# RWKV-7 recurrence in a hybrid decoder layer: V products on 64 rows, alternated with U and Y products of the preceding chunk

## The chip, the cores and the metric

The kernel runs on one core of a Trainium2 chip. The metric is the device time of one execution in microseconds. PE is TensorE (PEld its weight loads), DVE VectorE, ACT ScalarE, POOL GpSimd, and SP the engine whose queue issues most transfers.

## What is computed

One decoder layer on 1024 tokens of width 1024: a SwiGLU block, a mixer of two parallel groups of eight heads (stick-breaking attention and RWKV-7 time mixing), and a second SwiGLU block, each between RMS norms. The change lies in the RWKV-7 recurrence:

```python
def rwkv7_scan(r, w, k, v, a_vec, b_vec):
    """State S_h (N_v, N_k):
    S_t = S_{t-1} diag(w_t) + (S_{t-1} a_t) b_t^T + v_t k_t^T ;  y_t = S_t r_t."""
...
    def step(state, inp):
        r_t, w_t, k_t, v_t, a_t, b_t = inp
        sa = jnp.einsum('bhij,bhj->bhi', state, a_t)
        state = (state * w_t[:, :, None, :]
                 + sa[..., None] * b_t[:, :, None, :]
                 + v_t[..., None] * k_t[:, :, None, :])
        y = jnp.einsum('bhij,bhj->bhi', state, r_t)
        return state, y
```

## The kernel before

The layer runs in stages: first SwiGLU block, input projections, then the recurrence together with most of the attention, output projection with the rest of the attention, second SwiGLU block.

The recurrence does not step token by token. The 1024 tokens are cut into 16 chunks of 64 (`ch`, four to a quarter `q`). Earlier stages have written to DRAM, for each chunk, the operands A (`a_d`), M (`m_d`), B transposed (`bt_d`), a solved triangular matrix (`tt_d`) and the values V (`vt_d`). `chain_load(ch)` brings four of them in, three buffers each, on SP's queue. In the tile `UV` rows 64 to 127 are V, and rows 0 to 63 are set to zero by GpSimd (L1217) and later filled with U.

`rw_chain(q)` then does, for each chunk, with heads in four pairs `pr` of two heads `hd`:

1. V products (L1265): eight matmuls of M (128 rows, 128 columns as weights) with UV, 64 columns each, into the PSUM bank `gy`. UV's first 64 rows are zero at this time.
2. A products (L1268): four matmuls of A with the state S, added onto the same bank; then GpSimd scales the state (`sw`, L1271).
3. ScalarE copies gy's first 64 partitions to G (L1273).
4. U products (L1277): eight 64x64 matmuls of TT with G into a bank `us`; ScalarE copies the result to UV's first 64 rows (L1279).
5. S products (L1282): four matmuls of B with the whole of UV into another bank `us`; VectorE adds `sw` and writes the new state (L1286).
6. Y products (L1289): eight 64x64 matmuls of M's first 64 rows with U, added onto gy's last 64 partitions; ScalarE copies them out (L1292).

Each float32 matmul appears in the trace as two passes, each a weight load (LDWEIGHTS) and a MATMUL.

`rw_post(q)`, once per quarter, normalises the outputs and transposes them through two banks `us` (L1316), which VectorE reads (L1319). Attention (`att_s1` to `att_s4`: Z products L1392, mask L1395, transposes L1418, O products L1430) is written between the chunks by `pull`. A scheduler then orders each engine's instructions by its own estimate of when they are ready; `keep_in_program_order` ties an instruction behind the one written before it on its engine. Each engine runs its instructions in that fixed order.

PSUM has eight banks, given out by `PB_`: gy 1, us 2, z 2, at 2, po 1. `pcol` and `pc` pick the columns of a head or a pair of heads.

Of the kernel before, what the change touches and what calls it, by code (L numbers as in the profile page):

```python
# [30 lines left out]
def layer_kernel(ctx: ExitStack, tc: tile.TileContext, a: dict, out: bass.AP, dbg=None):  # L31
    nc = tc.nc
# [44 lines left out]
    def bank(tag, name):  # L77
        return PS.p.tile([P, 512], F32, tag=tag, name=name, bufs=PS.bufs[tag])
# [652 lines left out]
    v_d = dr.tile([T, 512], F32, name="v_d")  # L731
    yh_d = dr.tile([D, T], F32, name="yh_d")
    yl_d = dr.tile([D, T], F32, name="yl_d")
    PB_ = dict(gy=1, us=2, z=2, at=2, po=1)
    a_d = dr.tile([16, P, 4, P], F32, name="a_d")
    m_d = dr.tile([16, P, 4, 2, P], F32, name="m_d")
    bt_d = dr.tile([16, P, 4, P], F32, name="bt_d")
    tt_d = dr.tile([16, 64, 4, P], F32, name="tt_d")
# [129 lines left out]

    pm = Pool("ms", dict(qk=3, tmp=1, sl=1, L=1, TT=1))
    pl = Pool("ma", dict(t2=14, e65=4, ab=2, M=2))  # L870
    C4 = 4
# [143 lines left out]
    def rw_build(q, h):  # L1015
        pr, AB = q.pr, q.AB[h]
        odd = pr % 2
        if h == 0:
            if not odd:
                slabs[0] = pm.tile("sl", f"slab{pr}", [P, 32, 32])  # L1020
                slabs[1] = pm.tile("TT", f"TT{pr}", [P, 32, 64])
        bk = []
# [45 lines left out]
    def rw_solve(qs):  # L1068
        u = qs[0].pr
        slab, TT = slabs  # L1070
        L = pm.tile("L", f"L{u}", [P, 32, 32])
# [12 lines left out]
        nc.vector.transpose(TN, L.rearrange("p i j -> p j i"))  # L1084
        nc.vector.transpose(TT[:, :, 0:32].rearrange("p r i -> p i r"), L)
        for i in range(2):
            nc.gpsimd.memset(TT[kb[i][1], :, 32:64], 0.0)
        yield 6.0
        for hf in range(2):
            h16 = slice(hf * 16, hf * 16 + 16)  # L1090
            rr = range(hf * 16, hf * 16 + 16)
            for i in range(2):
                k0_, k1_ = kb[i]
                psy = bank("A", f"psy{u + i}{hf}")
                for x_, r in enumerate(rr):
                    nc.tensor.matmul(psy[k1_, x_ * 32:(x_ + 1) * 32], lhsT=TT[k0_, r, 32:64], rhs=TN[k0_, :, r],
                                     start=True, stop=True)
# [79 lines left out]
    for pr in range(4):  # L1177
        q = Pair()
# [23 lines left out]
    pb = Pool("mb", dict(A=3, M=3, bt=3, UV=3, TT=3, G=2, sw=2, Y=4, yg=3))  # L1202
# [3 lines left out]
    chain = {}  # L1206

    def chain_load(ch):
        cn = f"ch{ch}"
        A_ = pb.t2(cn + "A", [P, 4, P], tag="A")  # L1210
        nc.sync.dma_start(A_, a_d[ch])
        M = pb.t4(cn + "M", [P, 4, 2, P], tag="M")
        nc.sync.dma_start(M, m_d[ch])
        BT = pb.tile("bt", cn + "bt", [P, 4, P])
        nc.sync.dma_start(BT, bt_d[ch])
        UV = pb.tile("UV", f"{cn}UV", [P, 512])
        nc.gpsimd.memset(UV[0:64], 0.0)  # L1217
        nc.sync.dma_start(UV[64:128], vt_d[ch * 64:(ch + 1) * 64, :])
        chain[ch] = A_, M, BT, UV

    for ch in range(3):
        chain_load(ch)
# [3 lines left out]
    XP[0].close()  # L1226
    PS.open("psb", PB_)
    pa = Pool("at", dict(qk=6, V=1, p2=9, b2=3, O=2), "right")
# [15 lines left out]
    pcol = lambda pr, hd: slice(pr * P + hd * 64, pr * P + (hd + 1) * 64)  # L1244
    pc = lambda pr: slice(pr * P, (pr + 1) * P)

    def rw_chain(q):
        q.Y = pb.t4(q.nm + "Y", [P, 2, 512], tag="Y")
        for c in range(C4):
            S, Sn = S2[SCUR[0]], S2[1 - SCUR[0]]  # L1250
            SCUR[0] = 1 - SCUR[0]
            cn = f"{q.nm}c{c}"
            ch = q.qd * C4 + c
            if ch not in chain:
                chain_load(ch)
            A_, M, BT, UV = chain.pop(ch)
            TT = pb.tile("TT", cn + "TT", [64, 4, 2, 64])
            nc.sync.dma_start(TT[0:32].rearrange("p r h e -> p r (h e)"), tt_d[ch, 0:32])
            for o in range(2):
                nc.sync.dma_start(TT[32:64, :, :, o * 32:o * 32 + 32].rearrange("p r h e -> p (r h) e"),  # L1260
                                  tt_d[ch, 32:64].rearrange("p r (h o e) -> p (r h) o e", h=2, o=2)[:, :, 1 - o, :])
            gy = bank("gy", cn + "gy")
            for pr in range(4):
                for hd in range(2):
                    nc.tensor.matmul(gy[:, pcol(pr, hd)], lhsT=M[:, pr, hd, :], rhs=UV[:, pcol(pr, hd)],  # L1265
                                     start=pr == 0 and hd == 0, stop=True, skip_group_check=True)
            for pr in range(4):
                nc.tensor.matmul(gy[:, pc(pr)], lhsT=A_[:, pr, :],  # L1268
                                 rhs=S[:, pr, :], start=False, stop=True, skip_group_check=True)
            sw = pb.tile("sw", cn + "sw", [P, 4, P])  # L1270
            nc.gpsimd.tensor_tensor(sw, S, WC[:, :, ch:ch + 1].broadcast_to([P, 4, P]), op=ALU.mult)  # L1271
            G = pb.tile("G", cn + "G", [64, 512])
            nc.scalar.copy(G, gy[0:64, :])  # L1273
            u = bank("us", cn + "u")
            for pr in range(4):
                for hd in range(2):
                    nc.tensor.matmul(u[0:64, pcol(pr, hd)], lhsT=TT[:, pr, hd, :],  # L1277
                                     rhs=G[:, pcol(pr, hd)], start=True, stop=True)
            nc.scalar.copy(UV[0:64, :], u[0:64, :])  # L1279
            s = bank("us", cn + "s")  # L1280
            for pr in range(4):
                nc.tensor.matmul(s[:, pc(pr)], lhsT=BT[:, pr, :], rhs=UV[:, pc(pr)], start=True, stop=True)  # L1282
            sv = s.rearrange("p (r e) -> p r e", e=P)
            for hd in range(2):
                o = slice(hd * 64, (hd + 1) * 64)
                nc.vector.tensor_tensor(Sn[o, :, o], sv[o, :, o], sw[o, :, o], op=ALU.add)  # L1286
            for pr in range(4):
                for hd in range(2):
                    nc.tensor.matmul(gy[64:128, pcol(pr, hd)], lhsT=M[0:64, pr, hd, 64:128],  # L1289
                                     rhs=UV[0:64, pcol(pr, hd)], start=False, stop=True, skip_group_check=True)  # L1290
            ys = slice((c % 2) * 64, (c % 2) * 64 + 64)
            nc.scalar.copy(q.Y[ys, c // 2, :], gy[64:128, :])  # L1292
            yield 5.0
# [36 lines left out]
    def rwkv():  # L1330
        qs = []
        for qd in range(4):
            q = Quarter()
            q.qd, q.nm = qd, f"w{qd}"
            qs.append(q)
        for qd in range(4):
            for c, w in enumerate(rw_chain(qs[qd])):
                yield w
                if c == 0 and qd > 0:
                    yield from rw_post(qs[qd - 1])  # L1340
        yield from rw_post(qs[3])
# [243 lines left out]
```

## Time and profile before

| what | value |
| --- | --- |
| median of 3 runs | 2215.29 us (2211.8 to 2218.39) |
| the profiled execution | 2211.98 us |
| its span in the trace | 2210.3 us |
| PE busy | 2094.5 us (95%) |
| DVE, ACT, POOL busy | 1329.6, 817.2, 1108.3 us |
| mean granted PE clock | 0.976 of full speed |
| the recurrence | about 1120 to 1375 us of the span |

Busy times are sums of the durations of an engine's instructions; passes of PE overlap one another, so the pace of a group is read from where the next one starts. Times in the trace count from the span's start. The groups of rows that are used stand below.

### The profile page before, as it was taken

Reading aid. Unit: us, or ns where it says so; the run is one execution under the profiler, and the core shown is the slowest. Engines: PE = TensorE matmul, PEld = TensorE weight load, DVE = VectorE, ACT = ScalarE, POOL = GpSimd, SP = SyncE. Lnnn points to the kernel's source line nnn. Section 1 sums busy time; section 2 is a strip of 40 time slices with the busy share of each in tenths; the row PEclk is TensorE's granted clock in tenths of the full one; section 3 lists DMA queues with packets and bytes.
Section 4 is the critical chain, followed back from the end, with each engine's and each line's share of the span. In section 5 each row is a group of like instructions: output and inputs, shape, how many; then the busy total and the mean of one; then the engine's idle time right before and its main releaser. Section 6 shows DMA issues by size and latency. Waiting matters only on the chain.

```text
span 2210.3 us, 30206 instructions
## 1 busy us (share of the span) xinstructions
PE 2094.5 (95%) x10976; PEld 1719.9 (78%) x10976; DVE 1329.6 (60%) x1873; ACT 817.2 (37%) x1412; POOL 1108.3 (50%) x897
## 2 busy tenths in 40 slices
PE   8899999989999999999999999898799999998998
PEld 6678888868887777687888887777678888877886
DVE  7667777624546545735537778546676767733556
ACT  5233333332105533324136667436323333332102
POOL 2866666658542345245211111221686666647734
PEclk9999999999999999999989999999899999999999
DMA  5244555568764355164665572443235555566765
GB/s 153 76 124 130 164 141 157 153 213 307 225 215 146 78 168 172 48 181 140 192 150 159 174 217 87 157 129 115 76 100 149 161 153 146 160 225 204 254 212 190
DMA packets 415476, 353.82 MB, mean 160 GB/s; under 512 B 35169, under 2 KB 337249, under 8 KB 415329
## 3 DMA queue, kind: packets, MB, share of 16 engines
q1 hardware_dynamic: 406800, 347.45, 52.3%
q10 hardware_dynamic: 8528, 4.46, 0.9%
q8 instruction: 87, 1.43, 0.3%
q14 instruction: 61, 0.49, 0.1%
HBM read 224.96 MB, written 126.88 MB: 159 GB/s over the span
## 4 chain that ended last, share of the span: by engine, by line
PE 76%; DVE 9%; issue 4%; ACT 4%; POOL 4%; DMA 2%; SPq 0%; DVEq 0%; ACTq 0%; POOLq 0%
PE pj L124 3%; PE pj L126 2%; PE pj L125 2%; PE f2X L124 2%; PE f1X L124 2%; PE f2X L125 2%; PE f2X L126 2%; PE f1X L126 2%; PE f1X L125 2%; PE a_512o L1430 2%; PE f2DY L125 2%; PE f1DY L125 2%; PE f2DY L124 2%; PE f1DY L126 2%; PE f2DY L126 2%
## 5 line engine op out<-in xcount | busy, mean ns | idle before, releaser
L112 POOL TENSOR_SCALAR wh<-wr 128x1024 fp32r<-128x1024 f32 x54 | 62.3, 1155 | 280.1 <-PE wod L126 66.1
L319 POOL TENSOR_TENSOR f1wl<-f1r,f1wh 128x512 fp32r<-128x512 f32 x100 | 141.2, 1424 | 15.9 <-ACT f1wh L316 12.7
L319 POOL TENSOR_TENSOR f2wl<-f2r,f2wh 128x512 fp32r<-128x512 f32 x100 | 139.3, 1406 | 13.0 <-ACT f2wh L316 9.7
L113 POOL TENSOR_TENSOR wl<-wr,wh 128x1024 fp32r<-128x1024 f32 x54 | 136.6, 2532 | 3.1 <-PE pj L126 0.2
L318 POOL TENSOR_SCALAR f2wh<-f2r 128x512 fp32r<-128x512 f32 x60 | 68.5, 1147 | 107.4 <-PE f2pX L125 38.8
L318 POOL TENSOR_SCALAR f1wh<-f1r 128x512 fp32r<-128x512 f32 x60 | 60.0, 1005 | 91.6 <-PE f1X L125 27.0
L511 DVE TENSOR_TENSOR f1acc<-f1dX,f1acc 128x512 f32<-128x512 f32 x64 | 44.3, 692 | 76.8 <-PE f1dX L126 76.8
L511 DVE TENSOR_TENSOR f2acc<-f2dX,f2acc 128x512 f32<-128x512 f32 x64 | 44.3, 692 | 76.5 <-PE f2dX L126 76.5
L1409 POOL TENSOR_SCALAR a_0B<-a_512B 128x1 f32<-128x1 f32 x32 | 15.4, 482 | 131.4 <-DVE a_512B L1410 98.8
L124 PE MATMUL pj<-x1X4h,wh 128*128 128x512 f32 x176 | 75.5, 429 | 0.5 <-DVE tw L925 0.5
L124 PE MATMUL pj<-x1X2h,wh 128*128 128x512 f32 x176 | 72.3, 411 | 0.6 <-DVE qkl L1120 0.5
L126 PE MATMUL pj<-x1X4h,wl 128*128 128x512 f32 x176 | 70.5, 401 | 0.0
L125 PE MATMUL pj<-x1X4l,wh 128*128 128x512 f32 x176 | 69.6, 396 | 0.0
L125 PE MATMUL pj<-x1X2l,wh 128*128 128x512 f32 x176 | 69.4, 395 | 0.0
L126 PE MATMUL pj<-x1X2h,wl 128*128 128x512 f32 x176 | 69.4, 394 | 0.0
L319 POOL TENSOR_TENSOR f1wl<-f1S,f1wh 128x512 fp32r<-128x512 f32 x40 | 63.1, 1587 | 1.6
L319 POOL TENSOR_TENSOR f2wl<-f2S,f2wh 128x512 fp32r<-128x512 f32 x40 | 62.4, 1569 | 1.7
L537 POOL TENSOR_TENSOR f2dwl<-f2B,f2dwh 128x1024 fp32r<-128x1024 f32 x20 | 47.6, 2406 | 20.0 <-ACT f2dwh L536 20.0
L537 POOL TENSOR_TENSOR f1dwl<-f1B,f1dwh 128x1024 fp32r<-128x1024 f32 x20 | 47.6, 2401 | 19.4 <-ACT f1dwh L536 19.4
L124 PE MATMUL wod<-wh,ymh 128*128 128x512 f32 x128 | 51.6, 403 | 1.1 <-DVE woacc L196 1.1
L126 PE MATMUL wod<-wh,yml 128*128 128x512 f32 x128 | 50.2, 395 | 0.6 <-DMA yml<-yl_d 0.6
L125 PE MATMUL wod<-wl,ymh 128*128 128x512 f32 x128 | 50.4, 394 | 0.0
(1448 smaller groups left out, 7098.7 us busy)
## 6 DMA issues: line engine op xcount, KB each, us to landing
f1ho<-f1hs_d SPq DMA_DIRECT2D x112, 256.0 KB, 4.6
f2ho<-f2hs_d SPq DMA_DIRECT2D x112, 256.0 KB, 4.0
f1hs_d<-f1h SPq DMA_DIRECT2D x56, 256.0 KB, 3.3
f1hs_d<-f1l SPq DMA_DIRECT2D x56, 256.0 KB, 3.0
f2hs_d<-f2h SPq DMA_DIRECT2D x56, 256.0 KB, 3.0
f2hs_d<-f2l SPq DMA_DIRECT2D x56, 256.0 KB, 2.9
wr<-in_w_in_dram SPq DMA_DIRECT2D x27, 512.0 KB, 3.9
f1r<-in_ffn_w_gate_dram SPq DMA_DIRECT2D x19, 512.0 KB, 4.9
```

The costliest lines, as they stand in the source:

```text
L112: nc.gpsimd.tensor_scalar(wh, raw, 1.0, 0.0, op0=ALU.mult, op1=ALU.add)
L113: nc.gpsimd.tensor_tensor(wl, raw, wh, op=ALU.subtract)
L124: nc.tensor.matmul(ps, lhsT=lh, rhs=rh, start=first, stop=False, **kw)
L125: nc.tensor.matmul(ps, lhsT=lh, rhs=rl, start=False, stop=False, **kw)
L126: nc.tensor.matmul(ps, lhsT=ll, rhs=rh, start=False, stop=last, **kw)
L318: nc.gpsimd.tensor_scalar(wh, src[n], 1.0, 0.0, op0=ALU.mult, op1=ALU.add)
L319: nc.gpsimd.tensor_tensor(wl, src[n], wh, op=ALU.subtract)
L511: nc.vector.tensor_tensor(quarter(tt, n), ps, quarter(tt, n), op=ALU.add)
L537: nc.gpsimd.tensor_tensor(wl, src[n], wh, op=ALU.subtract)
L1409: nc.gpsimd.tensor_scalar(B[:, w:w + 1], iv, 1.0, 0.0, op0=ALU.mult, op1=ALU.add)
L1430: nc.tensor.matmul(po[:, 0:P], lhsT=t.AT[:, k * P:(k + 1) * P], rhs=V[:, t.z0 // P + k, :], start=t.first and k == 0, stop=t.last and k == ...
```

## The change

V products use V's 64 rows and M's rows 64 to 127 alone, so UV's first 64 rows need not be zero and the memset goes. Opening a chunk (loads, gy bank, V products) becomes a generator, `rw_open`. While chunk `ch` issues its U products, the first, third, fifth and seventh are each followed by one V product of chunk `ch + 1`, and so again with its Y products. V lies on rows 64 to 127, U and Y products on rows 0 to 63. `pin` holds this order. Chunk 0 has its V products ahead, as before. gy gets two banks, us one.

```diff
--- before.py
+++ after.py
@@ -731,7 +731,7 @@
     v_d = dr.tile([T, 512], F32, name="v_d")
     yh_d = dr.tile([D, T], F32, name="yh_d")
     yl_d = dr.tile([D, T], F32, name="yl_d")
-    PB_ = dict(gy=1, us=2, z=2, at=2, po=1)
+    PB_ = dict(gy=2, us=1, z=2, at=2, po=1)
     a_d = dr.tile([16, P, 4, P], F32, name="a_d")
     m_d = dr.tile([16, P, 4, 2, P], F32, name="m_d")
     bt_d = dr.tile([16, P, 4, P], F32, name="bt_d")
@@ -1214,7 +1214,6 @@
         BT = pb.tile("bt", cn + "bt", [P, 4, P])
         nc.sync.dma_start(BT, bt_d[ch])
         UV = pb.tile("UV", f"{cn}UV", [P, 512])
-        nc.gpsimd.memset(UV[0:64], 0.0)
         nc.sync.dma_start(UV[64:128], vt_d[ch * 64:(ch + 1) * 64, :])
         chain[ch] = A_, M, BT, UV
 
@@ -1244,26 +1243,41 @@
     pcol = lambda pr, hd: slice(pr * P + hd * 64, pr * P + (hd + 1) * 64)
     pc = lambda pr: slice(pr * P, (pr + 1) * P)
 
+    ops = {}
+    pin = tc.keep_in_program_order
+    hd8 = [(pr, hd) for pr in range(4) for hd in range(2)]
+
+    def rw_open(ch):
+
+        cn = f"ch{ch}"
+        if ch not in chain:
+            chain_load(ch)
+        A_, M, BT, UV = chain.pop(ch)
+        TT = pb.tile("TT", cn + "TT", [64, 4, 2, 64])
+        nc.sync.dma_start(TT[0:32].rearrange("p r h e -> p r (h e)"), tt_d[ch, 0:32])
+        for o in range(2):
+            nc.sync.dma_start(TT[32:64, :, :, o * 32:o * 32 + 32].rearrange("p r h e -> p (r h) e"),
+                              tt_d[ch, 32:64].rearrange("p r (h o e) -> p (r h) o e", h=2, o=2)[:, :, 1 - o, :])
+        gy = bank("gy", cn + "gy")
+        ops[ch] = A_, M, BT, UV, TT, gy
+        for j, (pr, hd) in enumerate(hd8):
+            i = nc.tensor.matmul(gy[:, pcol(pr, hd)], lhsT=M[64:128, pr, hd, :], rhs=UV[64:128, pcol(pr, hd)],
+                                 start=j == 0, stop=True, skip_group_check=True)
+            if ch:
+                pin(i)
+            yield
+
     def rw_chain(q):
         q.Y = pb.t4(q.nm + "Y", [P, 2, 512], tag="Y")
         for c in range(C4):
             S, Sn = S2[SCUR[0]], S2[1 - SCUR[0]]
             SCUR[0] = 1 - SCUR[0]
+            ch = q.qd * C4 + c
             cn = f"{q.nm}c{c}"
-            ch = q.qd * C4 + c
-            if ch not in chain:
-                chain_load(ch)
-            A_, M, BT, UV = chain.pop(ch)
-            TT = pb.tile("TT", cn + "TT", [64, 4, 2, 64])
-            nc.sync.dma_start(TT[0:32].rearrange("p r h e -> p r (h e)"), tt_d[ch, 0:32])
-            for o in range(2):
-                nc.sync.dma_start(TT[32:64, :, :, o * 32:o * 32 + 32].rearrange("p r h e -> p (r h) e"),
-                                  tt_d[ch, 32:64].rearrange("p r (h o e) -> p (r h) o e", h=2, o=2)[:, :, 1 - o, :])
-            gy = bank("gy", cn + "gy")
-            for pr in range(4):
-                for hd in range(2):
-                    nc.tensor.matmul(gy[:, pcol(pr, hd)], lhsT=M[:, pr, hd, :], rhs=UV[:, pcol(pr, hd)],
-                                     start=pr == 0 and hd == 0, stop=True, skip_group_check=True)
+            if ch not in ops:
+                for _ in rw_open(ch):
+                    pass
+            A_, M, BT, UV, TT, gy = ops.pop(ch)
             for pr in range(4):
                 nc.tensor.matmul(gy[:, pc(pr)], lhsT=A_[:, pr, :],
                                  rhs=S[:, pr, :], start=False, stop=True, skip_group_check=True)
@@ -1272,10 +1286,14 @@
             G = pb.tile("G", cn + "G", [64, 512])
             nc.scalar.copy(G, gy[0:64, :])
             u = bank("us", cn + "u")
-            for pr in range(4):
-                for hd in range(2):
-                    nc.tensor.matmul(u[0:64, pcol(pr, hd)], lhsT=TT[:, pr, hd, :],
+            ahead = rw_open(ch + 1) if ch < 15 else iter(())
+            for j, (pr, hd) in enumerate(hd8):
+                i = nc.tensor.matmul(u[0:64, pcol(pr, hd)], lhsT=TT[:, pr, hd, :],
                                      rhs=G[:, pcol(pr, hd)], start=True, stop=True)
+                if j:
+                    pin(i)
+                if j % 2 == 0:
+                    next(ahead, None)
             nc.scalar.copy(UV[0:64, :], u[0:64, :])
             s = bank("us", cn + "s")
             for pr in range(4):
@@ -1284,10 +1302,15 @@
             for hd in range(2):
                 o = slice(hd * 64, (hd + 1) * 64)
                 nc.vector.tensor_tensor(Sn[o, :, o], sv[o, :, o], sw[o, :, o], op=ALU.add)
-            for pr in range(4):
-                for hd in range(2):
-                    nc.tensor.matmul(gy[64:128, pcol(pr, hd)], lhsT=M[0:64, pr, hd, 64:128],
+            for j, (pr, hd) in enumerate(hd8):
+                i = nc.tensor.matmul(gy[64:128, pcol(pr, hd)], lhsT=M[0:64, pr, hd, 64:128],
                                      rhs=UV[0:64, pcol(pr, hd)], start=False, stop=True, skip_group_check=True)
+                if j:
+                    pin(i)
+                if j % 2 == 0:
+                    next(ahead, None)
+            for _ in ahead:
+                pass
             ys = slice((c % 2) * 64, (c % 2) * 64 + 64)
             nc.scalar.copy(q.Y[ys, c // 2, :], gy[64:128, :])
             yield 5.0
```

PE, chunk 4 (quarter 1, chunk 0) before: U (`w1c0u`), attention (names with `a_`), S and Y.

```order
L1277 MATMUL w1c0u<-w1c0G,w1c0TT 64x64 x8
L1430 MATMUL a_3_0o<-a00v,a_3_0AT 128x128 x2
L1392 MATMUL a_5_0z<-a01kh_d_9576,a01q 128x512
L1392 MATMUL a_5_0z<-a01kl_d_9579,a01q 128x512
L1282 MATMUL w1c0s<-ch4UV,ch4bt 128x128 x4
L1289 MATMUL w1c0gy<-ch4UV,ch4M 64x64 x8
L1418 MATMUL a_4_0t<-ident,a_4_0be 128x128 x4
```

The V products of chunk 5 come later, ahead of its A products:

```order
L1418 MATMUL a_6_0t<-ident,a_6_0be 128x128 x4
L1265 MATMUL w1c1gy<-ch5UV,ch5M 128x64 x8
L1268 MATMUL w1c1gy<-S_8460,ch5A 128x128 x4
L1316 MATMUL w0py_9981<-ident,w0Y 128x128 x4
L1430 MATMUL a_6_512o<-a00v,a_6_512AT 128x128 x3
L1316 MATMUL w0py_9987<-ident,w0Y 128x128 x4
```

PE, the same chunk after the change, from the last U products on; `ch5gy` with `ch5UV` is V of chunk 5.

```order
L1291 MATMUL w1c0u<-w1c0G,ch4TT 64x64 x2
L1264 MATMUL ch5gy<-ch5UV,ch5M 128x64
L1291 MATMUL w1c0u<-w1c0G,ch4TT 64x64
L1453 MATMUL a_3_0o<-a00v,a_3_0AT 128x128 x2
L1415 MATMUL a_5_0z<-a01kh_d_9594,a01q 128x512
L1415 MATMUL a_5_0z<-a01kl_d_9597,a01q 128x512
L1300 MATMUL w1c0s<-ch4UV,ch4bt 128x128 x4
L1306 MATMUL ch4gy<-ch4UV,ch4M 64x64
L1264 MATMUL ch5gy<-ch5UV,ch5M 128x64
L1306 MATMUL ch4gy<-ch4UV,ch4M 64x64 x2
```

Eight U products in a row have become single ones and pairs with a V product of chunk 5 (64 rows, which the row does not show; 128x64 is its output) between them, and the Y products likewise.

PE, the A products of chunk 5 after the change, with the transposes of the post step of quarter 0 (`w0py`) behind them:

```order
L1441 MATMUL a_6_0t<-ident,a_6_0be 128x128 x4
L1282 MATMUL ch5gy<-S_8460,ch5A 128x128 x4
L1339 MATMUL w0py_9997<-ident,w0Y 128x128 x4
L1453 MATMUL a_6_512o<-a00v,a_6_512AT 128x128 x3
L1415 MATMUL a_0_0z<-a10kh_d_10017,a10q 128x256
L1415 MATMUL a_0_0z<-a10kl_d_10020,a10q 128x256
L1339 MATMUL w0py_10003<-ident,w0Y 128x128 x4
```

The V products are gone from ahead of the A products, and two Z products of attention now stand between the two groups of transposes.

## Rows read from the trace of the kernel before

**Rows 1.** Page: engines' busy time, share and instructions; chain by engine.
```profile
PE 2094.5 (95%) x10976; PEld 1719.9 (78%) x10976; DVE 1329.6 (60%) x1873; ACT 817.2 (37%) x1412; POOL 1108.3 (50%) x897
...
PE 76%; DVE 9%; issue 4%; ACT 4%; POOL 4%; DMA 2%; SPq 0%; DVEq 0%; ACTq 0%; POOLq 0%
```

**Rows 2.** Busy time by stretch: the recurrence; columns are in the first line.
```profile
core 0: us, PE busy (x) PEld busy (x) DVE busy (x) ACT busy (x) POOL busy (x), PEclk, DMA share, GB/s
...
1120.00:1375.00 255.00, 237.17 (x2009) 208.99 (x2008) 176.21 (x314) 157.83 (x327) 46.14 (x117) 0.97 0.58 165
```

**Rows 3.** Chain in order of time, chunk 5: start, us, what.
```profile
1198.33 1.73 PE w1c1gy L1265 x16
```

**Rows 4.** Timeline of PE, chunk 5: start, us, what, passes.
```profile
1198.16 1.90 PE L1265 MATMUL w1c1gy<-ch5UV,ch5M 128*128 128x64 f32 x16
1199.90 1.11 PE L1268 MATMUL w1c1gy<-S,ch5A 128*128 128x128 f32 x8
1200.84 0.38 PE L1316 MATMUL w0py<-ident,w0Y 128*128 128x128 f32 x2
```

**Rows 5.** Timeline of PE, chunk 4, the Y block and what follows.
```profile
1189.14 1.14 PE L1289 MATMUL w1c0gy<-ch4UV,ch4M 64*64 64x64 f32 x16
1190.21 0.44 PE L1418 MATMUL a_0t<-ident,a_0be 128*128 128x128 f32 x2
```

**Rows 6.** Timeline, 1189.0 to 1189.2, then from 1190.06.
```profile
1188.82 0.39 PE L1282 MATMUL w1c0s<-ch4UV,ch4bt 128*128 128x128 f32 x2
...
1189.14 0.27 PE L1289 MATMUL w1c0gy<-ch4UV,ch4M 64*64 64x64 f32 x1
...
1189.89 0.39 PE L1289 MATMUL w1c0gy<-ch4UV,ch4M 64*64 64x64 f32 x4
```

**Rows 7.** Timeline, 757.0 to 757.8 and 786.5 to 788.0: 64-row matmuls on alternate halves.
```profile
757.15 0.69 PE L949 MATMUL r_0psd<-tw,W 64*128 64x512 f32 x1
...
757.16 0.69 PE L954 MATMUL r_0psa<-tw,W 64*128 64x512 f32 x1
...
786.72 1.16 PE L1043 MATMUL b000pm<-r_0AB 64*128 64x128 f32 x16
787.81 0.50 PE L124 MATMUL pj<-x1X4h,wh 128*128 128x512 f32 x1
```

**Rows 8.** Lines L1282, L1418, L1289, L1043: ns min/median/max, first and last start.
```profile
L1282 PE MATMUL w1c0s<-ch4UV,ch4bt x8: 273/275/275, 1188.2 to 1188.9; 128*128 128x128 f32 x8
...
L1418 PE MATMUL a_0t<-ident,a_0be x208: 270/273/448, 1143.7 to 1433.3; 128*128 128x128 f32 x104
...
L1289 PE MATMUL w1c1gy<-ch5UV,ch5M x16: 218/218/267, 1210.1 to 1211.0; 64*64 64x64 f32 x16
...
L1043 PE MATMUL b000pm<-r_0AB x16: 272/272/373, 786.7 to 787.6; 64*128 64x128 f32 x16
```

**Rows 9.** Tiles ch7UV and ch7M (landing in us), and the U block of chunk 6.
```profile
L1217 POOL MEMSET ch7UV<- x1: 517/517/517, 1190.4 to 1190.4; 64x512 f32 x1
...
L1213 SPq DMA_DIRECT2D ch7M<-m_d x1: 325/325/325, 1190.3 to 1190.3; - x1
...
DMA to landing us min/median/max: 3.9/3.9/3.9
...
1215.72 1.14 PE L1277 MATMUL w1c2u<-w1c2G,w1c2TT 64*64 64x64 f32 x16 [0.16 <-ACT w1c2G L1273]
```

**Rows 10.** Timeline of the post step of quarter 0, 1200.5 to 1203.0.
```profile
1201.48 0.69 DVE L1319 TENSOR_TENSOR w0yg<-w0py,w0gat 128x512 f32<-128x512 f32 x1 [0.53 <-PE w0py L1316]
...
1201.95 0.60 PE L1316 MATMUL w0py<-ident,w0Y 128*128 128x128 f32 x4
```

**Rows 11.** Clock: half the stretch (columns of rows 2), chain, a group of chunk 0.
```profile
1120.00:1250.00 130.00, 120.46 (x999) 106.47 (x999) 80.73 (x142) 73.52 (x155) 24.33 (x63) 0.93 0.62 174
...
1135.08 1.98 PE w0c1u L1277 x16
...
L1277 PE MATMUL w0c0u<-w0c0G,w0c0TT 64*64 64x64 f32 x16 | 1.1, 221 | 0.7 <-ACT w0c0G L1273 0.7
```

## The prediction

> **What bounds the kernel now.** I read the page first, then the stretch of the recurrence, then its chain, then single passes. The page [rows 1] gives TensorE 2094.5 of 2210.3 us, and 76% of the chain that ends last. The stretch from 1120 to 1375 us [rows 2], in which the sixteen chunks run with attention between them, says the same more sharply: PE is busy 237.2 of 255 us (93%), VectorE 176.2, ScalarE 157.8, GpSimd 46.1. So here a microsecond of PE is worth nearly a microsecond of the end, and the 17.8 us in which PE is idle are what can absorb a little. The chain [rows 3] shows the products with V (L1265) as pieces of 1.73 us, with the A products right behind them: they are on the path, not beside it. A float32 matmul appears as two passes, each with its own weight load, so eight matmuls are sixteen passes.
>
> What a pass costs is read from where the next group starts. V's sixteen passes, 128 rows by 128 columns of weights, run from 1198.16 to 1199.90 [rows 4]: 1.74 us, 0.109 each. The sixteen 64x64 passes of one Y block run from 1189.14 to 1190.21 [rows 5]: 1.07 us. The last four show the bare pace: they last 0.39 together, one alone 0.218, so three steps take 0.172, 0.057 each [rows 6]. A 128-row pass costs as much with 64 moving columns as with 128: the A products' eight passes take 0.94 [rows 4]. It is the load of 128 weight columns that sets it, so halving V's rows does not shorten its pass.
>
> **What the change takes out.** Fifteen of the sixteen V blocks leave their place ahead of the A products: 15 x 1.74 = 26.1 us of PE. Chunk 0's block stays, on 64 rows, at the same pace (zero).
>
> **What it puts in.** For chunks 0 to 14, each U block becomes U, V, U U, V, U U, V, U U, V, U, and the Y block the same, so 15 x 2 x 4 V matmuls return, with 64x128 weights on rows 64 to 127, between 64x64 weights on rows 0 to 63. What that costs depends on one thing that no row of this trace shows, because the two sizes never follow each other in it: what happens at such a neighbourhood. The bounds come from the two nearest kinds of row.
>
> *Lower end: the halves work at once.* Where two 64x128 matmuls lie on different halves and different banks, they do [rows 7]: psd starts at 757.15 and psa at 757.16. The sixteen passes of L1043, alternating halves one by one, take from 786.72 to 787.81, 1.09 us or 0.068 each, against 0.109 for one 128x128 pass. By these rows four V matmuls (8 x 0.109 = 0.87 us) fit under the 1.07 us of a U block and cost nothing.
>
> *Upper end: each change of size is paid.* Into a 64x64 block [rows 6, 8]: two L1282 passes start at 1188.82 and end 0.39 later, one lasts 0.275, so the last starts at 1188.935; the first 64x64 weights load at 1189.14, 0.205 later, where the regular step is 0.109: 0.096 lost. Its first pass takes 267 instead of 218 ns, since its weights were not loaded ahead: 0.049. Sum 0.145 us. Out of it: last pass at 1190.06, next weights at 1190.21, 0.15 instead of 0.057, and the first two L1418 passes take 0.44 instead of 0.11 + 0.273: 0.15 us again. Other blocks pay it too: their passes have 218 as median and 267 or more as maximum, those of the 64x128 groups 272 and 373 (one of each stands in [rows 8]; the others at full clock read alike).
>
> I take the upper end: 0.15 us per change. The new neighbours differ in weight columns (64 against 128) as well as in the half, so they are nearer to rows 6, where the size changes, than to rows 7, where size stays and only the half changes. The interleaving adds eight changes per block: 15 x 2 x 8 = 240. The V passes themselves then take 0.109 as now, so what was removed comes back (+26.1), and 240 x 0.15 = **36 us** of PE is added on top.
>
> [...]
>
> **The rest of the change.** The memset of UV's first 64 rows leaves GpSimd, 0.517 us a chunk [rows 9]. GpSimd is busy 46 of 255 us [rows 2] and chunk 7's memset, at 1190.4, stood far ahead of the V products that read it, which came after the U block of chunk 6 at 1215.72; so this is zero. The loads of the next chunk (A, M, bt, UV, TT) are now asked for one chunk earlier in the program, on the same SP queue. M of chunk 7 was issued at 1190.3 and takes 3.9 us to land [rows 9], while the U block of chunk 6, where it would now be read, starts at 1215.72 [rows 9]: some 21 us in hand, zero. Moved loads are late only if this shrinks to nothing. A second gy bank lets V write while the preceding Y accumulates; zero by itself. The us bank goes from two to one: U, S and the two transposes of the post step now follow each other in it. U to S waits for the ScalarE copy that S reads anyway, and the next U waits for the new state anyway. What is new is that the second transpose group must wait for VectorE's read of the first: it ends at 1201.48 + 0.69 = 1202.17, and the group started at 1201.95 [rows 10]. With the Z products that the new order puts ahead of it, this is covered; without them at most 0.69 us a quarter, 2.8 in all. I take 1. PE's queue is in order, so behind a V that waits stand the rest of U, and then ScalarE's copy and S.
>
> **Sum.** PE +36 us. Of this, PE's idle time (7% of the stretch) takes some up: it ends when VectorE or ScalarE deliver, and a PE that is later finds more of that ready. I pass on 0.9 (ends 0.8 and 1.0): +32.4, and +1 for the bank: +33. The profiled execution took 2211.98 us (span 2210.3), which gives 2245. The median of the three runs, 2215.29, lies 3.3 above it; on that the sum is 2248. I forecast **2247**. With the gap alone (0.09) and 0.8 passed on it is +17; with the whole 0.205 us per change +49: 2230 to 2262 on the median.
>
> **Rival 1: the halves overlap (faster).** The place is each U and Y block; it decides if PE starts a 64x128 pass on the upper half while 64x64 passes stream on the lower. For it: rows 7 show full overlap of halves, and the two halves write different banks. Against it: there both are of one size. Then 26.1 us of PE vanish; 0.8 passed on, as VectorE (69% busy) becomes the next limit, minus 1 for the bank: -20, 2195 on the median. If passes must also start in order, each V holds up a U pass by one load, 4 x 0.109 = 0.44 us a block, 13 us in all, and -9 is left. So -26 to -9: 2189 to 2206.
>
> [...]
>
> **Rival 2: neither.** The sizes follow each other without a gap and without overlap: 120 V matmuls x 2 x 0.109 come back, 26.2 against 26.1, no change, 2215. It would need the 0.15 us of rows 6 to come from the change of rows alone.
>
> [...]
>
> That V is not moved at all is excluded: the built order shows the alternation for all fifteen chunks.
>
> **How the numbers follow.** Changes of size paid (with or without rival 3): 0.63. Overlap: 0.27. Neither: 0.10. A measurement of this kernel can tell 0.3%, 6.6 us, from no change. Paid changes give slower in 0.61 of 0.63, the rest same; overlap gives faster in 0.26 of 0.27; neither is same in 0.08 and 0.01 to each side. So faster 0.27, same 0.11, slower 0.62. Cases of both signs hold most of the chance: the forecast's own range is 2230 to 2262; the range for 8 in 10 reaches into the overlap case, 2190 to 2260.
>
> **What would show it.** Right: in the profile after, a U block with its four V matmuls takes about 3 us from first to last start (1.07 + 0.87 + 8 x 0.15 = 3.1), the first 64x64 pass behind each V lasts about 267 ns, and PE's weight loads start only some 0.15 us after the last pass of the other size. Wrong: V and U passes start within 0.01 us of each other and the block stays near 1.1 to 1.5 us (rival 1), or the block takes 1.9 us with no gap (rival 2). If the stretch does not lengthen although blocks do, the 0.9 was wrong. If U waits for a load or for the us bank, the zeros of the rest were.

## The result and the profile after

The change made the kernel slower, by some 88 us where 33 were forecast: 2301.63 us as the median of 4 runs (2300.66 to 2306.71), against 2213.90 for the kernel before (4 runs). The ratio is 1.0395, 95% interval 1.0373 to 1.0417. The forecast was 2247, its range 2190 to 2260. The profiled execution took 2306.71 us, the highest of the four, with a span of 2305.0, so the spans differ by 94.7 us where the medians differ by 87.7.

First the page of the kernel after: busy time (as [rows 1]), the granted clock (the part of TensorE's full clock that it was given) in 40 slices of the span, in tenths, and the chain by engine.

```profile
PE 2184.6 (95%) x10976; PEld 1783.6 (77%) x10976; DVE 1329.8 (58%) x1873; ACT 818.4 (36%) x1412; POOL 1097.7 (48%) x881
...
PEclk9999999999999999999787978999899999999999
...
PE 78%; DVE 8%; issue 4%; POOL 4%; ACT 3%; DMA 2%; SPq 0%; DVEq 0%; POOLq 0%; ACTq 0%
```

PE has exactly as many passes as before (10976), but 90 us more of busy time, and the granted clock sags in the slices of the recurrence. The same stretch as [rows 2], then the recurrence itself, from the first V pass to ScalarE's last copy to Y, in the kernel after (columns as in rows 2):

```profile
1120.00:1375.00 255.00, 244.47 (x1480) 205.82 (x1480) 124.41 (x219) 111.71 (x230) 29.62 (x77) 0.77 0.45 129
...
1123.50:1456.00 332.50, 316.55 (x1967) 266.37 (x1966) 174.51 (x309) 155.32 (x319) 36.21 (x101) 0.79 0.43 126
```

And the recurrence of the kernel before:

```profile
1122.10:1371.80 249.70, 232.38 (x1974) 204.85 (x1973) 174.40 (x310) 154.78 (x321) 44.41 (x114) 0.97 0.59 167
```

The same 255 us first: PE starts 1480 passes in them instead of 2009, and is "busier", 244.5 against 237.2 us. The recurrence of either kernel, the last two rows, holds the same work but for a few passes of attention (1967 and 1974 passes): it takes 332.5 instead of 249.7 us, 82.8 more. PE's busy time in it grows by 84.2, and its idle time stays (16.0 against 17.3 us). Of the 94.7 us of span, 82.8 are therefore here; 1.4 come before it, 7.9 in the output projection (below), and the rest, 2.6, lies scattered behind.

Where they go inside the recurrence shows in single blocks. Timeline of PE in the kernel after (start, us, line, passes), part of a U block at half clock, then one at full clock:

```profile
1143.77 0.68 PE L1291 MATMUL w0c1u<-w0c1G,ch1TT 64*64 64x64 f32 x4
1144.38 0.68 PE L1264 MATMUL ch2gy<-ch2UV,ch2M 64*128 64x64 f32 x2
1144.99 0.68 PE L1291 MATMUL w0c1u<-w0c1G,ch1TT 64*64 64x64 f32 x4
...
1191.19 0.33 PE L1291 MATMUL w0c3u<-w0c3G,ch3TT 64*64 64x64 f32 x2
1191.44 0.43 PE L1264 MATMUL ch4gy<-ch4UV,ch4M 64*128 64x64 f32 x2
1191.81 0.44 PE L1291 MATMUL w0c3u<-w0c3G,ch3TT 64*64 64x64 f32 x4
1192.18 0.43 PE L1264 MATMUL ch4gy<-ch4UV,ch4M 64*128 64x64 f32 x2
1192.54 0.44 PE L1291 MATMUL w0c3u<-w0c3G,ch3TT 64*64 64x64 f32 x4
...
1194.01 0.33 PE L1291 MATMUL w0c3u<-w0c3G,ch3TT 64*64 64x64 f32 x2
```

The lower block is the forecast's own: U and V never share a moment, and four U and two V passes take 0.73 us (1191.81 to 1192.54), where bare paces and two holes of 0.15 give 4 x 0.057 + 2 x 0.109 + 0.30 = 0.75. The block lasts 3 us, as forecast, and the first pass behind each V lasts 267 ns, its weights loading 0.15 to 0.20 us after the last pass of the other size began. The upper one does the same in 1.22 us (1143.77 to 1144.99). That the clock is the difference is seen by tile, durations in ns (minimum, median, maximum), first and last start:

```profile
L1291 PE MATMUL w0c3u<-w0c3G,ch3TT x16: 218/218/267, 1191.2 to 1194.1; 64*64 64x64 f32 x16
...
L1291 PE MATMUL w0c1u<-w0c1G,ch1TT x16: 311/311/363, 1142.7 to 1147.6; 64*64 64x64 f32 x16
```

and by the granted clock of 10 us pieces of the same trace (columns as in rows 2, the clock third from the end; 0.50 is half clock throughout, 1.00 is full clock):

```profile
1130.00:1140.00 10.00, 9.33 (x42) 7.51 (x42) 0.84 (x2) 0.58 (x1) 1.05 (x1) 0.50 0.51 125
...
1210.00:1220.00 10.00, 10.00 (x45) 8.29 (x45) 2.94 (x5) 2.16 (x4) 1.54 (x1) 0.50 0.01 2
...
1230.00:1240.00 10.00, 9.85 (x78) 8.31 (x77) 9.50 (x16) 7.25 (x16) 0.61 (x6) 1.00 0.64 202
```

From 1210 to 1220 PE is "busy" 10.00 of 10 us, at half clock, with 45 passes where a piece at full clock has 78. The mix of work differs between the two, but the busy share shows nothing of the clock. It hides the holes too: the V passes that start at 1191.44 count as busy until 1191.87, though U has begun at 1191.81. By the records of the granted clock PE ran 139.9 us of the recurrence at half clock, against 17.1 before; the rounded 0.79 says the same: (1 - 0.79) / 0.5 x 332.5 = 140.

Last, the output projection. Waits of PE from 1488 to 1605 us in the kernel after (us in total, times, longest):

```profile
PE wod L124 <- ACT woacc L194: 4.7, 8, 0.7
```

In the kernel before PE has no such wait in its projection. The projection's first group takes its PSUM banks from the tag `us` as well, named in a table far from the recurrence; with one such bank PE waited for ScalarE's copies of its results, eight times and 4.7 us in all. From first to last pass the projection takes 113.4 us (1488.9 to 1602.3) against 105.5 (1404.1 to 1509.6).

### The profile page after: what moved, and what is told of

It reads as the page before. It is cut to its first block, busy times and chain, and to the rows that moved or that the text cites. A ratio compares the mean times of both kernels' runs of the same rounds, so it can differ in the third digit from the quotient of the medians.

```text
span 2305.0 us, 30162 instructions
## 1 busy us (share of the span) xinstructions
PE 2184.6 (95%) x10976; PEld 1783.6 (77%) x10976; DVE 1329.8 (58%) x1873; ACT 818.4 (36%) x1412; POOL 1097.7 (48%) x881
## 4 chain that ended last, share of the span: by engine, by line
PE 78%; DVE 8%; issue 4%; POOL 4%; ACT 3%; DMA 2%; SPq 0%; DVEq 0%; POOLq 0%; ACTq 0%
PE pj L124 3%; PE pj L126 2%; PE pj L125 2%; PE f2X L124 2%; PE f1X L124 2%; PE f1X L125 2%; PE f1X L126 2%; PE f2X L125 2%; PE f2X L126 2%; PE a_512o L1453 2%; PE f1DY L125 1%; PE f1DY L124 1%; PE f2DY L124 1%; PE f2DY L126 1%; PE f2DY L125 1%
## 5 line engine op out<-in xcount | busy, mean ns | idle before, releaser
L1433 DVE TENSOR_TENSOR_SCAN a_0B<-a_0nk,a_512B 128x512 f32<-128x512 f32 x32 | 45.1, 1410 | 9.8 <-ACT a_0nk L1421 9.7
```

The lines of the kernel that those rows point to most:

```text
L1433: nc.vector.tensor_tensor_scan(B[:, 0:w][:, ::-1], t.nk[:, 0:w][:, ::-1], t.nk[:, 0:w][:, ::-1], iv, op0=ALU.mult, op1=ALU.bypass)
```

## Experiments

In the expectations theory A is the forecast's step, that each change of tile size is paid; the other letters are explained where they stand. "Changes" are changes of tile size between successive passes of PE, counted over the whole trace: 150 before, 395 after.

**V on 64 rows in its old place.** The kernel before without the memset, and V's matmuls with 64x128 weights:

```diff
-        nc.gpsimd.memset(UV[0:64], 0.0)
...
-                    nc.tensor.matmul(gy[:, pcol(pr, hd)], lhsT=M[:, pr, hd, :], rhs=UV[:, pcol(pr, hd)],
+                    nc.tensor.matmul(gy[:, pcol(pr, hd)], lhsT=M[64:128, pr, hd, :], rhs=UV[64:128, pcol(pr, hd)],
```

> Kernel before, with one part of the change: V products on 64 rows and no memset, at their old place (one group of eight ahead of the A products), banks as before. Theory A (each change of tile size is paid, and the holes lower the clock): two changes of size a chunk in place of one more stretch of 128 rows, 32 x 0.15 to 0.2 us = 5 to 6 us of PE, ratio to before 1.001 to 1.004, mean granted clock 0.97 to 0.98. Theory B (it is the alternation of the row halves that costs, whatever the sizes): no change, ratio 0.999 to 1.001. Theory C (64-row V products by themselves make PE less active and lower the clock): clock clearly below 0.97 and ratio above 1.005.

Measured 2227.51 us, ratio 1.0069 (1.0052 to 1.0086). The recurrence, columns as before:

```profile
1118.70:1385.20 266.50, 252.23 (x1973) 219.44 (x1972) 173.84 (x310) 155.15 (x320) 38.62 (x101) 0.91 0.55 157
```

No matmul moves and no pass is added, yet the recurrence takes 16.8 us more. There are 56 changes more (206), since V's passes now differ in size from the 128x128 passes on either side, and attention's passes split some of V's groups. The direction is A's, the size above A's: 56 x 0.15 is 8.4. The granted clock, 0.91 for 0.97, points to the rest. The ratio is one that theory C gives too; the next experiment and the grouped version below speak against C.

**All of one size.** The change, but each V matmul cut into two 64x64 pieces, one behind every U and every Y product (shown for V; the two lines `if j % 2 == 0` go):

```diff
-            i = nc.tensor.matmul(gy[:, pcol(pr, hd)], lhsT=M[64:128, pr, hd, :], rhs=UV[64:128, pcol(pr, hd)],
-                                 start=j == 0, stop=True, skip_group_check=True)
+            for o in range(2):
+                i = nc.tensor.matmul(gy[o * 64:o * 64 + 64, pcol(pr, hd)], lhsT=M[64:128, pr, hd, o * 64:o * 64 + 64],
+                                     rhs=UV[64:128, pcol(pr, hd)], start=j == 0, stop=True, skip_group_check=True)
```

> The change, with each V product cut into two of 64 weight columns, so that V, U and Y all have 64x64 tiles; they still alternate one by one between the two row halves (U, V, U, V ...: 16 changes of half a block, none of size). Theory A: V streams beside U and Y, a block takes about 1.1 us, 26 us of PE go, ratio to before 0.988 to 0.996, clock at least 0.96. Theory B: at least as many alternations as in the change, so ratio 1.03 or more. Theory C: clock near 0.95 and ratio above 1.01.

Measured 2202.77 us, ratio 0.9956 (0.994 to 0.9972). Window of the recurrence:

```profile
1119.00:1350.20 231.20, 201.79 (x2223) 172.50 (x2223) 174.11 (x309) 153.51 (x319) 37.01 (x101) 0.99 0.64 181
```

and timeline of PE in a U block with its V pieces:

```profile
1195.14 0.27 PE L1292 MATMUL w1c1u<-w1c1G,ch5TT 64*64 64x64 f32 x1
1195.15 0.28 PE L1265 MATMUL ch6gy<-ch6UV,ch6M 64*64 64x64 f32 x2
...
1195.31 0.22 PE L1292 MATMUL w1c1u<-w1c1G,ch5TT 64*64 64x64 f32 x1
1195.31 0.27 PE L1265 MATMUL ch6gy<-ch6UV,ch6M 64*64 64x64 f32 x1
...
1196.01 0.28 PE L1292 MATMUL w1c1u<-w1c1G,ch5TT 64*64 64x64 f32 x2
1196.21 0.50 PE L1414 MATMUL a_0z<-a10kh_d,a10q 128*128 128x512 f32 x1
```

U and V start within 0.01 us of each other, and the block with V in it lasts 1.07 us (1195.14 to 1196.21), as long as one without. This is rival 1, and here it took one tile size: 64x64 beside 64x128, above, shared no moment. Alternation, banks and pins are as in the change; with the added changes of size gone (158 are left), 101 us of its recurrence go, and 3.4 us are at half clock instead of 139.9. There are more passes than in the change (11232 in the trace against 10976) and less PE busy time than in the kernel before: 201.8 us against 232.4. Against before the window falls by 18.5 only, as PE's idle time grows from 17.3 to 29.4 us, and some 6 of the 18.5 belong to the second gy bank (below).

**Fewer changes.** The change, but V's four matmuls together behind the fourth U and the fourth Y product (shown for U):

```diff
-                if j % 2 == 0:
-                    next(ahead, None)
+                if j == 3:
+                    for _ in range(4):
+                        next(ahead, None)
```

> The change, with the same products in the order four U, four V, four U (and four Y, four V, four Y): two added changes of size a block in place of eight, 60 in place of 240. Theory A: 60 x 0.15 to 0.2 = 9 to 12 us of PE and a clock that falls far less, 0.965 to 0.976, ratio 1.003 to 1.012. Theory C: clock near 0.95, ratio above 1.03. Theory B expects the same as A here (two alternations a block).

Measured 2245.88 us, ratio 1.0145 (1.0126 to 1.0164), above A's upper end and far below C. There are 220 changes. The recurrence:

```profile
1121.50:1395.70 274.20, 257.22 (x1967) 222.68 (x1967) 173.46 (x309) 153.86 (x319) 36.25 (x101) 0.91 0.53 152
```

**One neighbour of V's size.** The change, but the Y products use 128 weight columns as V does. Their first 64 result partitions land in the half of gy that ScalarE has read already, so the outputs stay the same.

```diff
-                i = nc.tensor.matmul(gy[64:128, pcol(pr, hd)], lhsT=M[0:64, pr, hd, 64:128],
+                i = nc.tensor.matmul(gy[:, pcol(pr, hd)], lhsT=M[0:64, pr, hd, :],
```

> The change, with the Y products on 128 weight columns instead of 64 (the first 64 outputs land in a part of the bank that nobody reads afterwards), so that Y and V have the same size 64x128 and U keeps 64x64. Half of the 240 changes of size are gone; Y passes cost 0.109 instead of 0.057 (+0.67 us a block, 11 us). Theory A: Y blocks take about 1.8 us with V streaming beside them, U blocks stay at 3.1 or more; ratio to before 1.008 to 1.025, clock between 0.955 and 0.97. Theory B: nothing gained, ratio 1.035 or more.

Measured 2272.38 us, ratio 1.0269 (1.0247 to 1.0291), slightly above A's range. There are 287 changes. The recurrence, and the timeline of PE in a Y block:

```profile
1120.30:1422.70 302.40, 285.82 (x1973) 244.49 (x1973) 175.96 (x310) 154.87 (x321) 37.23 (x101) 0.85 0.48 138
...
1173.08 0.27 PE L1306 MATMUL ch2gy<-ch2UV,ch2M 64*128 64x64 f32 x1
1173.09 0.27 PE L1264 MATMUL ch3gy<-ch3UV,ch3M 64*128 64x64 f32 x1
1173.19 0.27 PE L1306 MATMUL ch2gy<-ch2UV,ch2M 64*128 64x64 f32 x1
1173.20 0.32 PE L1264 MATMUL ch3gy<-ch3UV,ch3M 64*128 64x64 f32 x1
```

Y on rows 0 to 63 and V on rows 64 to 127 start together here, 0.11 us a step. So the other half of the rows costs nothing here; it is the number of weight columns, 64 against 128, that makes the hole. Y's passes are twice as slow this way (0.109 for 0.057, or 0.83 us a block), but V beside them costs nothing (0.87 us a block), so these two cancel, and the kernel is faster than the change.

**Is it the passes or their neighbours that lower the clock?** The 64x64 pieces of V, but as one group behind Y, without alternation: both `next(ahead, None)` lines go.

> The same-size kernel with V not alternated: the next chunk's V products, 64x64, stand in one group behind the Y products (no added change of size, no half beside another). It tells what lowers the clock. Theory D (the holes at changes of size): half-clock time in the recurrence stays near 17 to 25 us, V is serial again (32 x 0.057 = 1.83 against 1.74 us a chunk, +1.4 us) and with the output projection's 8 us the ratio is 1.002 to 1.007. Theory E (64-row passes by themselves count as little work): half-clock time as in the run with V on 64 rows alone (48 us) or more, ratio 1.010 or more.

Measured 2208.46 us, ratio 0.9969 (0.9958 to 0.998). The recurrence takes 236.6 us at a granted clock of 0.97, with 160 changes and 13.7 us at half clock (17.1 before). That is far from theory E: there are as many half-row passes as with alternation, and the clock stays. Theory D is right about the clock, which fell even less than it says, but the ratio is below its range: V's group is not serial, as the last timeline of this section shows.

**The two kinds of bank alone.** The kernel before with `gy=2, us=1`, nothing else:

> Kernel before with the banks alone changed: gy two, us one. If the us bank of the output projection costs what it seems to: +6 to +9 us, ratio 1.003 to 1.004, the wod group 112 to 114 us from first to last instead of 105.5, recurrence within 3 us of before. If the longer output projection of the change has another cause: ratio 0.999 to 1.001.

Measured 2217.28 us, ratio 1.0009 (1.0000 to 1.0017). This is the ratio of the second case, but as the sum of two terms. From first to last pass the projection takes 113.2 us (1396.2 to 1509.4), 7.7 more than before. But the recurrence takes 243.8 instead of 249.7 us, and I had no such term:

```profile
1119.20:1363.00 243.80, 227.35 (x1968) 200.77 (x1967) 173.23 (x309) 153.09 (x319) 41.19 (x114) 0.99 0.61 171
```

The difference shows at the start of the recurrence, where there is no attention yet to fill in: PE's timeline in the banks-alone kernel whose projection is moved too (below; its recurrence is the same):

```profile
1124.69 1.11 PE L1268 MATMUL w0c0gy<-S,ch0A 128*128 128x128 f32 x8
1125.64 1.45 PE L1265 MATMUL w0c1gy<-ch1UV,ch1M 128*128 128x64 f32 x12
1127.02 1.14 PE L1277 MATMUL w0c0u<-w0c0G,w0c0TT 64*64 64x64 f32 x16
```

V of chunk 1 goes into the second bank while U of chunk 0 still waits for ScalarE's G. In the kernel before PE waits there, 0.7 us ahead of U [rows 11], and from 1132 to 1146 us it is at half clock; here the granted clock is 1.00 from 1120 to 1145 us, and the recurrence has 3.4 us at half clock instead of 17.1. That the wait is what lowers the clock fits this, but no run shows it by itself.

**The change with the projection on the gy banks.**

```diff
-        ([yblk(k) for k in (4, 5, 6, 7)], lambda q, n: wo_v[:, 4 + q:6 + q, n * 512:(n + 1) * 512], "us", "t"),
+        ([yblk(k) for k in (4, 5, 6, 7)], lambda q, n: wo_v[:, 4 + q:6 + q, n * 512:(n + 1) * 512], "gy", "t"),
```

> The change itself, with the first group of the output projection in the two gy banks. If the bank term is separate from the changes of size: 6 to 9 us under the change, some 2292 to 2296, ratio 1.035 to 1.0375. Rival as for the same-size kernel: ratio 1.039 to 1.041.

Measured 2290.55 us, ratio 1.0331 (1.0307 to 1.0355): 11 us under the change's median, slightly more than forecast. The recurrence is unchanged (332.6 us, granted clock 0.79, again 139.9 us at half clock), and the projection is back, from 1487.9 to 1592.1 us (columns as by tile above):

```profile
L124 PE MATMUL wod<-wh,ymh x128: 387/389/622, 1487.9 to 1591.6; 128*128 128x512 f32 x128
...
L126 PE MATMUL wod<-wh,yml x128: 387/389/501, 1488.8 to 1592.1; 128*128 128x512 f32 x128
```

So this term is separate from the recurrence. In the four pairs of kernels that differ by this edit alone (three of them below) the projection takes 113.2 to 113.8 us on the us bank and 104.2 to 104.5 on the gy banks, some 9 us; the ratios of the pairs differ by 4 to 14 us.

**Versions that beat both.** The same edit of the projection on three kernels: the alternated 64x64 version, the banks alone, and the grouped 64x64 version.

> The same-size kernel (V, U and Y all 64x64, alternated), with the first group of the output projection in the two gy banks instead of the one us bank. Theory: the us bank that the change takes away is also the output projection's, whose PE now waits for ScalarE's copy eight times (4.7 us in the trace of the change) and takes 8 us longer from first to last. Then this is 6 to 9 us under the same-size kernel: ratio to before 0.990 to 0.994, faster than both kernels. Rival: the output projection is longer because attention ends earlier and leaves it without company; then no gain, ratio 0.995 to 0.997.

> The kernel before with two gy banks and one us bank, and the first group of the output projection on the gy banks; every matmul of the recurrence is as before. Theory F (the second gy bank lets V of the next chunk run ahead, and this is worth about 6 us whatever V's rows are): the recurrence takes 243 to 246 us (before 249.7), the output projection 104 to 106 again, ratio 0.996 to 0.998. Theory G (the gain of the same-size version came from the 64-row halves working at once, the banks alone give nothing): recurrence 248 to 251, ratio 0.999 to 1.001.

> V in 64x64 pieces in a group behind Y (no alternation), two gy banks, one us bank, first group of the output projection on the gy banks. If alternating one by one is worth nothing beyond what the group gets by overlapping Y's end: ratio 0.993 to 0.995, as the alternated version with the same banks (0.9938). If the alternation itself gains: 0.996 to 0.998, level with the kernel that changes the banks alone.

| version | median us | ratio (95% interval) | recurrence us |
| --- | --- | --- | --- |
| banks alone | 2208.25 | 0.9971 (0.996 to 0.9981) | 243.7 |
| V 64x64, alternated | 2201.12 | 0.9938 (0.9925 to 0.9951) | 238.0 |
| V 64x64, grouped behind Y | 2195.77 | 0.9914 (0.99 to 0.9927) | 236.8 |

All three are under 1% faster than the kernel before, each with its whole interval below 1. The second bank gives its 6 us with V's 128 rows too (theory F). The 64x64 pieces take the median another 7 to 12 us down. The grouped version came out below its forecast (0.993 to 0.995), and alternating shows no gain over grouping: with the projection on the us bank the order of the two is the other way (0.9956 alternated, 0.9969 grouped). A single profile of the recurrence does not settle it either. The alternated version's, with the same passes in the same order, took 231.2 us above and takes 238.0 here, with 3.4 and 10.2 us at half clock. Why a group does about as well is in the timeline of the grouped version, at the end of Y of chunk 5:

```profile
1198.58 0.27 PE L1265 MATMUL ch6gy<-ch6UV,ch6M 64*64 64x64 f32 x2
...
1198.75 0.22 PE L1305 MATMUL ch5gy<-ch5UV,ch5M 64*64 64x64 f32 x1
1198.75 0.98 PE L1265 MATMUL ch6gy<-ch6UV,ch6M 64*64 64x64 f32 x27
1199.66 1.05 PE L1283 MATMUL ch6gy<-S,ch6A 128*128 128x128 f32 x7
```

V's 32 passes take 1.08 us up to the A products, against 1.74 for its 16 wide ones [rows 4]: the two 64x64 pieces of one V matmul lie on the same rows and on different columns, and they overlapped one another too: 1.08 / 32 is 0.034 us a pass, against 0.057 for the 64x64 passes of one Y block [rows 6]. Over the recurrence PE is busy 216.46 us with grouping and 205.25 with alternation, but idle 20.3 against 32.8: what alternation takes off PE's busy time comes back as idle time.

## Why the prediction was wrong in size

**What held.** PE bounds the stretch: its busy time grew by 84.2 us and the window by 82.8. I passed on 0.9; 0.98 was nearer, since PE's idle time did not shrink. A 128-column pass cost about 0.11 on half the rows too (the step of wide Y). The choice of the upper end, "each change of size is paid" at 0.15 us, held: the full-clock block took 0.73 us per round against 0.75, and it vanished where the sizes are the same. By that term the 245 changes added give 37 us. The loads asked for a chunk earlier stayed free: no transfer stands among PE's waits in the recurrence. Rival 1 (the halves overlap) fell for 64x64 beside 64x128 and is right for equal sizes; its price, 26.1 us of which some 20 reach the end, was too high. Against the recurrence with the same banks (243.8 us) the alternated one-size version gains 6 to 13 us. A slip in the sum: the inner range of 2230 to 2262 is added to the profiled execution, and on the median it lies some 3 us higher.

In the trace of the kernel after a change of size costs 0.15 us, and the version with wide Y shows what the trace of before could not: from one half to the other, a change of columns makes the hole (two of 0.15 in the 0.73 us of a round of U and V), and with equal columns there is none (Y and V at 0.11 us a step). Passes on different halves overlapped at equal size only: U and V of 64x64, like Y and V of 64x128, start within 0.01 us of each other.

**The step that failed: the price of the clock (rival 3).** I left a lower clock out of the sum. In the kernel before the U block of chunk 1 took 1.98 us [rows 11], against 1.07 for as many passes at full clock [rows 5]; the granted clock around it was 0.50 (columns as in rows 2):

```profile
1135.00:1140.00 5.00, 4.20 (x26) 3.82 (x27) 0.00 (x0) 2.51 (x6) 0.00 (x0) 0.50 1.06 219
```

One more stretch like that was to cost, by my estimate, 5 to 8 us. It was not one stretch: 139.9 instead of 17.1 us of the recurrence ran at half clock. Of such a microsecond 0.40 is lost, by the two rounds above (0.73 against 1.22 us). So 122.8 x 0.40 = 49 us, more than the holes themselves. Half of the 122.8 us would be 61; the two rounds show less.

Holes and clock together reproduce the four versions with changes of size. The first is set against the kernel before (150 changes, 17.1 us at half clock, recurrence 249.7), the others, which have two gy banks, against the banks alone (162 changes, 3.4 us, 243.8):

| version | changes added x 0.15 | half clock added x 0.40 | sum | measured |
| --- | --- | --- | --- | --- |
| V on 64 rows in place | 56: 8.4 | 30.7: 12.3 | 20.7 | 16.8 |
| groups of four | 58: 8.7 | 47.8: 19.1 | 27.8 | 30.4 |
| wide Y | 125: 18.8 | 88.8: 35.5 | 54.3 | 58.6 |
| the change | 233: 35.0 | 136.5: 54.6 | 89.6 | 88.7 |

The split is worked out, not run by itself: no version had the changes without the lower clock. A second count from the traces of before and after agrees with it. Take each pass of the recurrence from its start to the start of the next: at the pace of its full-clock stretches the change takes 36 us more than the kernel before, 28 of them in U, V and Y passes (127 against 91 ns each), and its slower passes at half clock add another 46 us (U, V and Y 219 against 127 ns, attention 237 against 151).

In all four versions more time at half clock comes with more changes, from 31 us for 56 changes to 137 for 233, and the versions of one size stay at 3.4 to 13.7 us. It does not go block by block: of the 768 U, V and Y passes of the change, 500 started at full clock, the lower block above among them. What in a change makes the chip lower the clock stays open.

**The second step: the us bank.** "At most 2.8" looked at the recurrence and its post step alone. In the output projection, which takes its banks from the same tag, it cost 7.9 us. The second gy bank, which I had put at zero, gives 6 us by itself. Its 13.7 us less at half clock come to 5.5 of them, so it is contained in the 122.8 us above. Against the kernel before the terms are then: holes +37 (forecast +36), clock +49 (forecast at most 8, and that outside the sum), together 86 where the recurrence shows 82.8; projection +8 (forecast none).

## What to carry to other kernels

In these runs small matmuls on different halves of TensorE worked at once where their tiles had the same number of rows and columns (64x64 with 64x64, 64x128 with 64x128, starts 0.01 us apart); cut the wider one to the size of its neighbours before alternating, and look first whether a plain group of equal tiles does as well. Price a change of tile size at its hole and at the clock: where holes come in quick succession, look at the granted clock of that stretch (0.79 here, 0.97 before), since PE's busy share hides both (95% in both kernels). Before taking a bank from a tag, list every stage that draws from it (here the output projection, 7.9 us).

## What the runs showed that I had not expected

- PE at half clock can read as 100% busy: 45 passes in 10 us (1210 to 1220) at 0.50 of the clock, 78 (of another mix) at 1.00.
- Cutting V's 64x128 matmuls into two of 64x64 each made twice the passes and took less time: 32 passes in 1.08 us against 16 in 1.92 (1123.53 to 1125.45 us, chunk 0 of the kernel after) or, on 128 rows, in 1.74.
- Passes on different halves did not always start in program order: in the grouped version V's matmuls stand behind all of Y's, and V's first passes start at 1198.58, ahead of Y's last ones (1198.63 to 1198.75).
- With a second gy bank and the same matmuls the clock stayed up at the start of the recurrence: 3.4 us at half clock instead of 17.1.
